# A transformer layer on one core: TensorE multiplies ones into an unread bank ahead of its first transposes and after its first token tile

## The chip, the cores and the metric

The kernel runs on one core of a Trainium2 chip. That core has four compute engines that run side by side, each with its own queue, worked off in order: TensorE (PE in the profile; its weight loads are PEld), VectorE (DVE), ScalarE (ACT) and GpSimd (POOL). A fifth queue, SyncE (SP), issues most DMA transfers. Engines wait for one another through semaphores. The metric is the device time of one execution in microseconds, as the median of several runs.

## The reference

One layer on 1024 tokens with 1024 features, in float32:

```python
h = rmsnorm(x, g_mix)
z = h @ w_in                     # pooling channels | q | k | v
y_pool = pool_mixer(z[pool])     # trailing means over 2, 4, 8, 16 tokens
y_attn = diff_attention(q, k, v) # 8 heads, two softmax maps each
gates  = sigmoid(h @ w_gate + b_gate)
x = x + (gates_1 * (y_pool @ w_branch_pool) + gates_2 * (y_attn @ w_branch_attn)) @ w_out
x = x + square(relu(rmsnorm(x, g_ffn) @ w_up)) @ w_down
```

Only the first two lines and the start of the attention's first head lie where the change is made; the rest matters since TensorE works through it behind them.

## The kernel before, in words

Every float32 matrix is split in two parts, a rounded "hi" and the remainder "lo". A product is then three multiplications: hi by hi, hi by lo, lo by hi (`mm3`, L126 to L128). The split (`split`) is a cast on ScalarE (L120), which writes hi, and a subtraction behind it (L121) on VectorE or GpSimd, which writes lo.

The tokens are cut into 8 tiles `t` of 128. For each tile, `norm_x` and `norm_transpose` square the row `x` and sum it (L244 for tile 0, L252 for the others, ScalarE), form the scale `rs` (VectorE L234, GpSimd L235), scale the row in two halves `hn` (VectorE L256), transpose each half by four TensorE transposes into a PSUM bank `hps` (L261), and split each bank by twos into `hT`: `hT0` and `hT1` come from the first half's bank, `hT2` and `hT3` from the second's. The splits are ScalarE casts L120 and VectorE subtractions L121 out of that bank.

`stage_qkv` then multiplies a tile with the q, k and v weights of one head into the bank `z`: eight steps `k` of three multiplications over 384 columns, 24 in all; steps 0 and 1 read `hT0`, 2 and 3 `hT1`, 4 and 5 `hT2`, 6 and 7 `hT3`. The weights of the first head come by DMA in four pieces `rqkv`, and are split into eight `wqkv`: eight casts on ScalarE, with the subtractions of numbers 0, 1, 4 and 5 on GpSimd, and of 2, 3, 6 and 7 on VectorE. `stage_prep` squares `z` (`sq`, ScalarE L423), reduces it (`ms`, VectorE L424) and scales it (`qn`, L428); later stages make scores, softmax and the product with v.

In the names of the instruction order, `hps1_0` is the first half's bank of tile 1, `z0_1` is head 0, tile 1, and the last number is only a serial number. `hT` has no tile in its name: its tiles hold four token tiles each, and the bank that is read tells which.

What the engines do in which order is not written out by hand. The program gives each instruction a priority, mostly its place in the source; a scheduler in the framework then plays the program with its own estimates of durations, and fixes for each engine the order in which instructions became ready there. Whatever takes time on one engine in that play can thus move instructions on all the others. On the chip each queue then runs in the fixed order.

## Time and profile before

| | us |
|---|---|
| time, median of 3 runs | 1529.52 (1528.83 to 1530.18) |
| the profiled execution's own time | 1529.71 |
| its span, first to last instruction | 1527.6 |
| TensorE busy | 1509.7 (99%) |
| VectorE, ScalarE, GpSimd busy | 1048.5, 804.7, 319.8 |
| TensorE's first multiplication starts | 8.75 |
| granted TensorE clock, mean over the span | 0.999 |

A row of the timeline holds the start, the time from the start of the first to the end of the last merged instruction, engine, line, operation, result and operands, the shape and the count, and in brackets how long the engine sat idle before and what ended that. Multiplications are pipelined: the distance from one start to the next is what one costs, not its duration. In rows of windows, each engine has its busy time and, in brackets, its instructions; PEclk is the clock that TensorE was granted, as a share of full speed.

### The profile page before, as it was taken

To read this page: it belongs to the slowest core of one execution; us is meant where nothing else is said; L and a number is where in the kernel's file an instruction comes from. 1 tells how busy PE (TensorE), PEld (TensorE's weight loads), DVE (VectorE), ACT (ScalarE), POOL (GpSimd) and SP (SyncE) were. 2 spreads that over 40 slices of the span, in tenths; PEclk is the share of its full clock that TensorE was granted. 3 is DMA by queue.
4 is the path that set the end of the run, shared out by engine and by line. 5 is a ranking of instruction groups with operands and counts; after the bars stand their busy time and mean duration, and the time that the engine had idled before them with its cause. 6 is when DMAs were issued, how large, how long until landed. Compare 5 with 4: busy or idle time off the path is not lost.

```text
span 1527.6 us, 21675 instructions
## 1 busy us (share of the span) xinstructions
PE 1509.7 (99%) x7441; PEld 1302.0 (85%) x7441; DVE 1048.5 (69%) x2262; ACT 804.7 (53%) x1693; POOL 319.8 (21%) x412
## 2 busy tenths in 40 slices
PE   7999999999999999999999999999999999999998
PEld 6999999999898989888888888888888888888887
DVE  6776668777777777746578559766665668556572
ACT  6665556656565565454464466555555634333331
POOL 6687333335234242312100011000000000000000
PEclk9999999999999999999999999999999999999999
DMA  7253202112112131627365734554433799537750
GB/s 247 100 159 120 76 29 62 51 44 66 43 44 84 49 98 40 223 89 254 120 209 191 248 104 149 169 178 152 148 128 110 274 344 383 170 125 262 228 190 28
DMA packets 171608, 221.07 MB, mean 145 GB/s; under 512 B 10902, under 2 KB 104811, under 8 KB 171499
## 3 DMA queue, kind: packets, MB, share of 16 engines
q1 hardware_dynamic: 154090, 192.39, 38.0%
q10 hardware_dynamic: 17408, 27.30, 4.8%
q8 instruction: 59, 0.97, 0.3%
q14 instruction: 51, 0.41, 0.1%
HBM read 157.76 MB, written 61.90 MB: 144 GB/s over the span
## 4 chain that ended last, share of the span: by engine, by line
PE 95%; DVE 2%; DMA 1%; ACT 1%; SPq 1%; issue 0%; POOL 0%; DVEq 0%
PE z L126 6%; PE z L128 6%; PE z L127 6%; PE Da L126 4%; PE Da L128 4%; PE Da L127 4%; PE g L126 4%; PE g L127 4%; PE g L128 4%; PE Db L126 3%; PE Db L128 3%; PE Db L127 3%; PE X L128 3%; PE X L127 3%; PE X L126 3%; PE sc L484 2%
## 5 line engine op out<-in xcount | busy, mean ns | idle before, releaser
L126 PE MATMUL z<-wqkv,hT 128*128 128x384 f32 x512 | 174.9, 343 | 0.6 <-DVE qn L428 0.4
L128 PE MATMUL z<-wqkv,hT 128*128 128x384 f32 x512 | 173.7, 340 | 0.0
L127 PE MATMUL z<-wqkv,hT 128*128 128x384 f32 x512 | 173.5, 339 | 0.0
L495 ACT ACTIVATE s<-s,nm 128x256 f32<-128x256 f32 (+7 forms) x128 | 99.5, 778 | 46.5 <-DVE nm L487 45.6
L126 PE MATMUL g<-hT,fwgate 128*128 128x512 f32 x256 | 101.1, 395 | 0.1
L127 PE MATMUL g<-hT,fwgate 128*128 128x512 f32 x256 | 100.8, 394 | 0.0
L128 PE MATMUL g<-hT,fwgate 128*128 128x512 f32 x256 | 100.5, 393 | 0.0
L126 PEld LDWEIGHTS z<-wqkv,hT 128*128 128x128 f32 x512 | 96.8, 189 | 3.4 <-DVE qn L428 0.6
L127 PEld LDWEIGHTS z<-wqkv,hT 128*128 128x128 f32 x512 | 96.9, 189 | 3.1 <-POOL wqkv L121 0.2
L235 POOL TENSOR_TENSOR ms<-ms,mhalf 128x4 f32<-128x4 f32 x64 | 65.7, 1027 | 158.3 <-DVE ms L234 135.3
L128 PEld LDWEIGHTS z<-wqkv,hT 128*128 128x128 f32 x512 | 96.5, 189 | 2.5 <-DVE hT L121 0.3
L121 DVE TENSOR_TENSOR AT<-ta,AT 128x256 fp32r<-128x256 f32 (+1 forms) x160 | 62.2, 392 | 32.7 <-ACT AT L120 31.6
L487 DVE CUSTOM_DVE_ANT_0 s<-sc,dist 128x512 f32<-128x512 f32 (+3 forms) x128 | 73.9, 583 | 13.2 <-PE sc L485 12.1
L120 ACT CAST AT<-ta 128x256 fp32r<-128x256 f32 (+1 forms) x160 | 54.5, 347 | 37.9 <-PE ta L527 23.1
L484 PE MATMUL sc<-K,Q 128*128 128x512 f32 (+2 forms) x192 | 69.8, 365 | 0.5 <-DVE nm L487 0.5
L121 DVE TENSOR_TENSOR AS<-s,AS 128x512 fp32r<-128x512 f32 x64 | 44.1, 693 | 36.5 <-ACT AS L120 36.3
L485 PE MATMUL sc<-K,Q 128*128 128x512 f32 (+2 forms) x192 | 66.4, 350 | 0.0
L121 POOL TENSOR_TENSOR wqkv<-rqkv,wqkv 128x384 fp32r<-128x384 f32 x60 | 61.8, 1044 | 19.8 <-ACT wqkv L120 16.7
L121 POOL TENSOR_TENSOR fwgate<-frgate,fwgate 128x512 fp32r<-128x512 f32 x32 | 43.3, 1356 | 66.0 <-ACT fwgate L120 66.0
L126 PEld LDWEIGHTS g<-hT,fwgate 128*128 128x128 f32 x256 | 48.1, 188 | 9.3 <-ACT go L730 0.5
L128 PEld LDWEIGHTS g<-hT,fwgate 128*128 128x128 f32 x256 | 48.1, 188 | 8.9
L127 PEld LDWEIGHTS g<-hT,fwgate 128*128 128x128 f32 x256 | 48.1, 188 | 8.4
(455 smaller groups left out, 4485.0 us busy)
## 6 DMA issues: line engine op xcount, KB each, us to landing
wd<-in_w_down_dram SPq DMA_DIRECT2D x56, 512.0 KB, 5.6
wu<-in_w_up_dram SPq DMA_DIRECT2D x32, 512.0 KB, 4.4
udS<-us SPq DMA_DIRECT2D x64, 256.0 KB, 2.4
ur<-udS SPq DMA_DIRECT2D x32, 512.0 KB, 3.4
rqkv<-in_w_in_dram SPq DMA_DIRECT2D x64, 192.0 KB, 2.7
ud<-u ACTq DMA_DIRECT2D x48, 256.0 KB, 4.1
ur<-ud SPq DMA_DIRECT2D x24, 512.0 KB, 4.3
frgate<-in_w_gate_dram SPq DMA_DIRECT2D x32, 256.0 KB, 2.8
```

What stands on the lines that cost most here:

```text
L120: nc.scalar.copy(hi, src)
L121: return (lo_eng or nc.vector).tensor_tensor(lo, src, f(hi), op=ALU.subtract)
L126: nc.tensor.matmul(ps, lhs_hi, rhs_hi, start=first, stop=False, **kw)
L127: nc.tensor.matmul(ps, lhs_hi, rhs_lo, start=False, stop=False, **kw)
L128: nc.tensor.matmul(ps, lhs_lo, rhs_hi, start=False, stop=last, **kw)
L235: nc.gpsimd.tensor_tensor(dst, dst, mhalf[:, :n], op=ALU.pow)
L484: nc.tensor.matmul(dst, Q[:, i, 0, :], rhs, start=True, stop=False)
L485: nc.tensor.matmul(dst, Q[:, i, 1, :], rhs, start=False, stop=True)
L487: nc.vector.tensor_tensor_reduce(out=s[i][:, c : c + w], in0=sc[:, 0:w], in1=dist[:, o0 + c : o0 + c + w], scale=2.0 ** -(h + 1), scalar=B ...
L495: nc.scalar.activation(s[i][:, 0:n], s[i][:, 0:n], AF.Exp, bias=last, scale=-1.0, accum_out=Z[:, i, t : t + 1])
```

## The change

A bank of the pool that later takes the attention's output is claimed early under the name `idle`. Nobody reads it. `keep_warm(n)` multiplies a 128x128 tile of ones into it n times, 512 columns each. It is called twice: with 22 ahead of everything that the start-up list `START` names, and with 7 behind the last multiplication of head 0, tile 0. `mm3` returns its last instruction for that purpose, and `issue_after` places the seven behind it.

```diff
-        nc.tensor.matmul(ps, lhs_lo, rhs_hi, start=False, stop=last, **kw)
+        return nc.tensor.matmul(ps, lhs_lo, rhs_hi, start=False, stop=last, **kw).ins
...
+        idle = ps_o.tile([P, 512], F32, tag="o", name="idle")
+
+        def keep_warm(n):
+            for _ in range(n):
+                nc.tensor.matmul(
+                    idle.rearrange("p (a b) -> p a b", a=4), ones, ones.unsqueeze(1).broadcast_to([P, 4, P]),
+                    start=True, stop=True,
+                )
+
+        keep_warm(22)
         for w in START.split():
...
-                mm3(z[:, 0:384], l_hi, l_lo, w[:, 0, :], w[:, 1, :], k == 0, k == NK - 1)
+                done = mm3(z[:, 0:384], l_hi, l_lo, w[:, 0, :], w[:, 1, :], k == 0, k == NK - 1)
+                if (h, t, k) == (0, 0, NK - 1):
+                    with tc.issue_after(done):
+                        keep_warm(7)
                 yield
```

The 29 multiplications are all that is added, and nothing is taken out. But the order moves on every engine, through the whole attention part (some 460 pieces of TensorE's order differ, nearly all within its first 4000 of 7441 multiplications). Three places matter to the prediction.

The first is ScalarE at the start, where it casts the first head's weights (`wqkv`) and tile 0's transposed rows (`hT` out of the banks `hps0_0` and `hps0_1`). Before:

```order
L120 CAST wqkv0_2_206<-rqkv0_1_189 128x384
L120 CAST hT0_0_0_150<-hps0_0_167 128x2x128
L120 CAST wqkv0_3_209<-rqkv0_1_189 128x384
L120 CAST wqkv0_4_214<-rqkv0_2_192 128x384
L120 CAST hT2_0_0_154<-hps0_1_177 128x2x128
L120 CAST hT1_0_0_152<-hps0_0_167 128x2x128
L120 CAST wqkv0_5_217<-rqkv0_2_192 128x384
L120 CAST wqkv0_6_220<-rqkv0_3_195 128x384
L120 CAST hT3_0_0_156<-hps0_1_177 128x2x128
L120 CAST wqkv0_7_223<-rqkv0_3_195 128x384
```

And now:

```order
L120 CAST wqkv0_2_229<-rqkv0_1_212 128x384
L120 CAST wqkv0_3_232<-rqkv0_1_212 128x384
L120 CAST wqkv0_4_237<-rqkv0_2_215 128x384
L120 CAST wqkv0_5_240<-rqkv0_2_215 128x384
L120 CAST hT0_0_0_173<-hps0_0_190 128x2x128
L120 CAST wqkv0_6_243<-rqkv0_3_218 128x384
L120 CAST hT2_0_0_177<-hps0_1_200 128x2x128
L120 CAST wqkv0_7_246<-rqkv0_3_218 128x384
L120 CAST hT1_0_0_175<-hps0_0_190 128x2x128
L120 CAST hT3_0_0_179<-hps0_1_200 128x2x128
```

The first cast of the rows moved behind three more weights, and `hT1`, which step 2 of the product reads, behind all eight.

The second is ScalarE from tile 1's square sum to tile 1's `hT1`. Before:

```order
L252 ACTIVATE hn1_248,ss1_249<-x1_198 128x1024
L252 ACTIVATE hn2_278,ss2_279<-x2_212 128x1024
L423 ACTIVATE sq0_0_431<-z0_0_372 128x256
L120 CAST hT0_0_0_150<-hps1_0_255 128x2x128
L120 CAST hT2_0_0_154<-hps1_1_265 128x2x128
L252 ACTIVATE hn3_304,ss3_305<-x3_226 128x1024
L120 CAST hT1_0_0_152<-hps1_0_255 128x2x128
```

And now:

```order
L252 ACTIVATE hn1_271,ss1_272<-x1_221 128x1024
L252 ACTIVATE hn2_301,ss2_302<-x2_235 128x1024
L436 ACTIVATE sq0_0_461<-z0_0_395 128x256
L391 ACTIVATE ls_264<-ls_264 128x2
L120 CAST hT0_0_0_173<-hps1_0_278 128x2x128
L120 CAST hT2_0_0_177<-hps1_1_288 128x2x128
L252 ACTIVATE hn3_327,ss3_328<-x3_249 128x1024
L252 ACTIVATE hn4_361,ss4_362<-x4_297 128x1024
L120 CAST hT0_0_0_173<-hps2_0_308 128x2x128
L120 CAST V0_0_391<-z0_0_395 128x128
L120 CAST hT1_0_0_175<-hps1_0_278 128x2x128
```

Tile 1's `hT1` moved behind tile 4's square sum, tile 2's `hT0` and the cast of v, and a small exponential (`ls`), whose operand VectorE reduces between the two halves of tile 2's `hn`, came ahead of tile 1's first cast.

The third is TensorE from the end of tile 0 to step 2 of tile 1. Before:

```order
L128 MATMUL z0_0_372<-wqkv0_7_223,hT3_0_1_157 128x384
L261 MATMUL hps1_0_255<-identf_96,hn1_248 128x128 x4
L261 MATMUL hps1_1_265<-identf_96,hn1_248 128x128 x4
L126 MATMUL z0_1_442<-wqkv0_0_200,hT0_0_0_150 128x384
L127 MATMUL z0_1_442<-wqkv0_0_200,hT0_0_0_150 128x384
L128 MATMUL z0_1_442<-wqkv0_0_200,hT0_0_1_151 128x384
L126 MATMUL z0_1_442<-wqkv0_1_203,hT0_0_0_150 128x384
L127 MATMUL z0_1_442<-wqkv0_1_203,hT0_0_0_150 128x384
L128 MATMUL z0_1_442<-wqkv0_1_203,hT0_0_1_151 128x384
L261 MATMUL hps2_0_285<-identf_96,hn2_278 128x128 x4
L126 MATMUL z0_1_442<-wqkv0_2_206,hT1_0_0_152 128x384
```

And now:

```order
L338 MATMUL idle_145<-ones_103 128x512 x7
L261 MATMUL hps1_0_278<-identf_96,hn1_271 128x128 x4
L261 MATMUL hps1_1_288<-identf_96,hn1_271 128x128 x4
L261 MATMUL hps2_0_308<-identf_96,hn2_301 128x128 x4
L126 MATMUL z0_1_472<-wqkv0_0_223,hT0_0_0_173 128x384
L127 MATMUL z0_1_472<-wqkv0_0_223,hT0_0_0_173 128x384
L261 MATMUL hps2_1_318<-identf_96,hn2_301 128x128 x4
L128 MATMUL z0_1_472<-wqkv0_0_223,hT0_0_1_174 128x384
L126 MATMUL z0_1_472<-wqkv0_1_226,hT0_0_0_173 128x384
L127 MATMUL z0_1_472<-wqkv0_1_226,hT0_0_0_173 128x384
L128 MATMUL z0_1_472<-wqkv0_1_226,hT0_0_1_174 128x384
L126 MATMUL z0_1_472<-wqkv0_2_229,hT1_0_0_175 128x384
```

The seven multiplications of ones stand between tile 0 and tile 1's transposes, and tile 2's first transposes moved ahead of all of tile 1's product.

## The prediction

> **What bounds the kernel now.** I read the page's busy times first, then TensorE's waits, the chain of waits at the start, and the timelines of the first 30 us.

> ```profile
> span 1527.6 us, 21675 instructions
> PE 1509.7 (99%) x7441; PEld 1302.0 (85%) x7441; DVE 1048.5 (69%) x2262; ACT 804.7 (53%) x1693; POOL 319.8 (21%) x412
> PE hps L261 <- DVE hn L256: 10.6, 2, 8.8
> PE X L128 <- DVE A L121: 0.9, 1, 0.9
> PE Y L126 <- DVE u L1246: 0.8, 1, 0.8
> PE Da L126 <- DVE u L1246: 0.5, 1, 0.5
> PE sc L484 <- DVE nm L487: 0.5, 1, 0.5
> PE z L126 <- DVE qn L428: 0.4, 1, 0.4
> ```

> The last six rows are TensorE's waits: total, times, longest. It waits 10.6 us for the first two tiles' rows and 0.9 + 0.8 + 0.5 + 0.5 + 0.4 = 3.1 us in all the rest. So from the second tile on the time is TensorE's own work, and each microsecond that TensorE starts this work later or wastes in it ends in the result.

> When that work starts is told by the chain of waits, and how fast by TensorE's timeline and three windows:

> ```profile
> 8.97 5.76 DMA x<-in_x_dram
> 14.75 1.16 ACT hn L252 x2
> ...
> 17.66 1.30 PE hps L261 x8
> ...
> 15.52 0.34 PE L128 MATMUL z<-wqkv,hT 128*128 128x384 f32 x1
> 18.75 0.69 PE L126 MATMUL z<-wqkv,hT 128*128 128x384 f32 x1
> 20.52 0.52 PE L128 MATMUL z<-wqkv,hT 128*128 128x384 f32 x1
> 20.84 1.05 PE L261 MATMUL hps<-identf,hn 128*128 128x128 f32 x4
> 21.55 0.67 PE L126 MATMUL z<-wqkv,hT 128*128 128x384 f32 x1
> 22.23 0.60 PE L261 MATMUL hps<-identf,hn 128*128 128x128 f32 x4
> 22.59 0.42 PE L128 MATMUL z<-wqkv,hT 128*128 128x384 f32 x1
> 23.02 0.34 PE L127 MATMUL z<-wqkv,hT 128*128 128x384 f32 x1
> 23.20 0.34 PE L128 MATMUL z<-wqkv,hT 128*128 128x384 f32 x1
> 26.84 1.47 PE L261 MATMUL hps<-identf,hn 128*128 128x128 f32 x12
> 28.07 0.42 PE L128 MATMUL z<-wqkv,hT 128*128 128x384 f32 x1
> ...
> 8.46:11.87 3.41, 3.12 (x12) 2.84 (x13) 2.65 (x5) 3.32 (x9) 2.81 (x3) 1.00 1.03 306
> 15.28:18.69 3.41, 1.61 (x12) 1.10 (x10) 2.08 (x7) 2.40 (x6) 0.87 (x2) 1.00 0.78 235
> 18.69:22.10 3.41, 3.41 (x14) 3.15 (x13) 3.19 (x12) 3.06 (x9) 3.26 (x5) 0.50 0.78 241
> ```

> Tile 1's row `x` lands at 14.75, and its norm lets the transposes start at 17.66. Tile 0's last multiplication started at 15.52 and ended at 15.86, so TensorE idles 1.8 us (15.86 to 17.66). Then it runs on, but from 18.69 to 22.10 at half clock (the last windows row, 0.50): six multiplications start from 18.75 to 20.84, 0.35 each at first and 0.32 at the end, where 23.02 to 23.20 shows 0.17 to 0.18.

> **The 22 ahead of the first transposes.** The ones are written early, and TensorE has nothing to do until the first half of `hn`:

> ```profile
> 0.90 0.20 POOL L218 MEMSET ones<- 128x128 f32 x1
> 8.75 1.97 PE L261 MATMUL hps<-identf,hn 128*128 128x128 f32 x8 [8.75 <-DVE hn L256]
> 32.30 0.39 PE L127 MATMUL g<-hT,fwgate 128*128 128x512 f32 x1
> 32.53 0.39 PE L128 MATMUL g<-hT,fwgate 128*128 128x512 f32 x1
> ```

> One of 512 columns costs 0.23 us at full clock (32.30 to 32.53); slow I take 0.32 x 512/384 = 0.43. From 1.1 on, 22 of them take 5.1 us if all are fast and 9.5 if all are slow. The slow stretch seen lasted 3.41 us, and where the switches fall need not be tied to the kernel's start; 8 slow and 14 fast give 1.1 + 3.4 + 3.2 = 7.7, before 8.75. At worst they run to 10.6 and push the transposes.

> Would that matter, or would earlier, faster transposes help? ScalarE answers both:

> ```profile
> 8.47 1.62 ACT L120 CAST wqkv<-rqkv 128x384 fp32r<-128x384 f32 x3 [4.17 <-DMA rqkv<-in_w_in_dram]
> 9.99 0.37 ACT L120 CAST hT<-hps 128x256 fp32r<-128x256 f32 x1
> 10.26 1.00 ACT L120 CAST wqkv<-rqkv 128x384 fp32r<-128x384 f32 x2
> 11.16 0.64 ACT L120 CAST hT<-hps 128x256 fp32r<-128x256 f32 x2
> 9.06 5.07 POOL L121 TENSOR_TENSOR wqkv<-rqkv,wqkv 128x384 fp32r<-128x384 f32 x4 [3.08 <-DMA rqkv<-in_w_in_dram]
> ```

> Before, three weights, then `hT0` at 9.99, ready at 10.36, and TensorE's first product at 10.41; `hT2` and `hT1` end at 11.80. A weight costs about 0.5, a row piece about 0.3. In the new order six weights precede `hT0`: 8.47 + 6 x 0.5 = 11.5, ready at 11.85, even if the transposes end as late as 11.4. So the speed of the first transposes buys nothing, and the product starts 1.45 later. `hT1` then comes behind `hT0`, a weight, `hT2` and a weight: 11.5 + 2 x 0.35 + 2 x 0.5 = 13.2, ready at 13.5 against 11.8. Its lo half, on VectorE behind three weights and two row pieces, I put at 14.6. From step 2's third multiplication there are 16 left, 16 x 0.17 = 2.8: tile 0 ends at 17.4, if slow for part of it 17.8, against 15.86. The fixed bound of before, GpSimd's subtractions until 14.13 (9.06 + 5.07), is no longer the last.

> **The seven after tile 0.** 7 x 0.23 = 1.6 us: 17.4 + 1.6 = 19.0, or 19.4. Tile 1's transposes, whose operand is ready at 17.6, so start 1.3 to 1.7 late. With tile 0 ending as before, at 15.9, they would end at 17.5 and cost nothing, under the cover of tile 1's norm.

> **Tile 1 behind them.** Here the moved order of ScalarE decides:

> ```profile
> 19.27 1.06 ACT L252 ACTIVATE hn<-x 128x1024 f32<-128x1024 f32 x1
> 20.32 0.36 ACT L120 CAST hT<-hps 128x256 fp32r<-128x256 f32 x1
> 20.57 1.07 ACT L252 ACTIVATE hn<-x 128x1024 f32<-128x1024 f32 x1
> 18.16 0.41 DVE L424 TENSOR_REDUCE ms<-sq 128x4 f32<-128x256 f32 x1
> 19.22 1.41 DVE L256 SCALAR_TENSOR_TENSOR hn<-x,rs,gmb 128x512 f32<-128x512 f32 x2
> 20.55 0.28 DVE L380 TENSOR_REDUCE ls<-lp 128x2 f32<-128x128 f32 x1
> ```

> VectorE starts the reduction `ms` of tile 0 at 18.16 before; now two small products stand ahead of it, which I put at 0.4. Behind them come `ms` (0.4), one half of `hn2` (0.7) and `ls` (0.2 to the next start): 19.85. ScalarE's exponential waits for that, 0.2: 20.05. Then `hT0` and `hT2` of tile 1 (20.75), the square sums of tiles 3 and 4 at 1.05 each (19.27 to 20.32): 22.8, `hT0` of tile 2 and v, 0.5, and `hT1` of tile 1 at 23.3, ready at 23.65. TensorE meanwhile does the transposes of tile 1 and tile 2 and steps 0 and 1 of tile 1, and is through at 22.2 to 22.5. It waits 1.2 to 1.4 us for `hT1`, behind which all the rest queues, whenever tile 0 ended. Step 2's first two run to 24.0. The same set of work was done before at 22.59: **1.4 us late.**

> After that the rows carry it: tile 2's product waits until `qn` of tile 0 has left its bank (I put it at 24.15), and by 29.6 TensorE has done what it had done at 28.07: 1.5 late. The stretch at half clock, in which the kernel before lost 6 x 0.15 = 0.9 on products, 0.35 on four transposes (20.84 to 21.55 against 22.23 to 22.59) and 0.3 on step 2 (two in 0.68, 21.55 to 22.23), is already inside this difference: the saving of 1.5 is real, and the late start (1.3 to 1.7) and the wait (1.2 to 1.4) eat it twice.

> Later, nothing is added. By the order the multiplications that stand between a tile's product and its transposes of q and k are 15 us of work at the least (12 before), and the groups of transposes 171 for 175, so I cost the moved remainder at nothing, between 3.1 less (all other waits gone) and 3.1 more (twice the waits).

> Sum: 1529.71 + 1.5 = 1531.2 for the profiled execution; the median lay 0.2 under it: **1531.0**.

> [...]

> **The rivals.**

> *It does what it says.* If the casts on ScalarE are early enough after all, transposes start at 17.66, no half clock follows, and 1.5 are saved: 1528.0. For it: the stretch of 0.50 is there to be saved. Against: two places of ScalarE's order. 18%.

> *The clock falls again.* The new wait before step 2 leaves TensorE idle for up to 1.4 us. In the window that fell, 1.61 of 3.41 were busy, transposes included, and it was followed by 3.4 us at half. If 22.2 to 23.6 lies in one window, about 1.9 of 3.41 are busy, not much more. Then another 1.6 are lost: 1532.6. [...] 15%; a little over half of it beyond 0.2%.

> *The moved remainder costs.* One mechanism: a square sum of a coming tile, or another early item, ahead of a cast that TensorE waits for, as at tile 1, on later tiles and heads. At 3.1 more: 1534.1, slower. Against it stands the cover above. 10%.

> *The moved remainder gains,* with the saving whole: down to 1529.5 - 1.5 - 3.1 = 1524.9. 5%.

> **How the numbers follow.** My forecast has 52%. A measurement of this kernel can tell about 0.2%, 3.1 us, from no change: 1526.5 to 1532.6 counts as the same. That holds the forecast (but for 2%), the first rival and less than half of the second: 0.74. Slower: 0.02 + 0.09 + 0.10 = 0.21. Faster: 0.05. The range from 1527.4 to 1533.3 leaves out most of the third and all of the fourth rival, some 13%, and a few per cent at the edges.

> **What would show it.** In the changed profile: the multiplications of ones end before 8.7; ScalarE's first `hT` cast starts near 11.5; tile 0's last product near 17.4; the seven end near 19; TensorE waits over 1 us before step 2 of tile 1, until about 23.6; no window at 0.50 between 18 and 22. The 12 transposes that began at 26.84 end 1.5 us later. It is wrong if the transposes of tile 1 start by 17.7, if a second stretch at half clock shows, or if TensorE's waits behind 30 us add up to much other than 3 us.

## The result, and the profile after

The changed kernel takes 1537.91 us (median of 6 runs, 1536.59 to 1538.21) against 1529.41 us for the kernel before (6 runs, 1528.35 to 1530.18): a ratio of 1.0054, with a 95% interval from 1.0041 to 1.0067. It is slower by 8.5 us. The forecast was 1531.0, within 1527.4 to 1533.3.

The page of the changed kernel, span and busy times, and then all of TensorE's waits of 0.8 us and more (total, times, longest):

```profile
span 1535.5 us, 21743 instructions
PE 1520.0 (99%) x7470; PEld 1308.5 (85%) x7470; DVE 1044.9 (68%) x2262; ACT 809.3 (53%) x1693; POOL 320.1 (21%) x412
PE z L126 <- ACT hT L120: 3.4, 2, 2.1
PE z L126 <- DVE qn L441: 1.6, 2, 1.3
PE idle L338 <- POOL ones L218: 1.2, 1, 1.2
PE hps L261 <- DVE hn L256: 1.0, 1, 1.0
PE X L128 <- DVE A L121: 0.9, 1, 0.9
PE Y L126 <- DVE u L1259: 0.8, 1, 0.8
```

The 10.6 us of waiting for the first two tiles' rows are down to 1.0, because the ones fill the first of these waits and a later end of tile 0 the second. In their place stand 3.4 us for casts of `hT` on ScalarE, a wait that the kernel before did not have, and 1.6 us for `qn` on VectorE, where it was 0.4. TensorE is busy 10.3 us longer (1520.0 for 1509.7), and the ones alone take 6.7 + 1.8 = 8.5 of that, as the next rows show.

TensorE's timeline at the start of the changed kernel:

```profile
1.16 6.71 PE L338 MATMUL idle<-ones 128*128 128x512 f32 x22 [1.16 <-POOL ones L218]
8.85 1.32 PE L261 MATMUL hps<-identf,hn 128*128 128x128 f32 x8 [0.99 <-DVE hn L256]
12.26 0.69 PE L126 MATMUL z<-wqkv,hT 128*128 128x384 f32 x1 [2.09 <-ACT hT L120]
17.40 0.52 PE L126 MATMUL z<-wqkv,hT 128*128 128x384 f32 x1
17.72 0.41 PE L127 MATMUL z<-wqkv,hT 128*128 128x384 f32 x1
...
19.03 0.33 PE L128 MATMUL z<-wqkv,hT 128*128 128x384 f32 x1
19.20 1.78 PE L338 MATMUL idle<-ones 128*128 128x512 f32 x7
20.82 1.47 PE L261 MATMUL hps<-identf,hn 128*128 128x128 f32 x12
25.11 0.44 PE L126 MATMUL z<-wqkv,hT 128*128 128x384 f32 x1 [1.32 <-ACT hT L120]
31.84 0.42 PE L128 MATMUL z<-wqkv,hT 128*128 128x384 f32 x1
```

Tile 0's product starts at 12.26, behind a wait of 2.09 us for the first cast, and up to 17.72 one multiplication costs 0.32 us (17.40 to 17.72), the half-clock price. It ends at 19.4 (19.03 + 0.33). The seven follow, tile 1's transposes start at 20.82, and before step 2 of tile 1 TensorE waits 1.32 us more. The last row is the multiplication that started at 28.07 before: here it starts at 31.84, **3.8 us late**. The span is 7.9 us longer in all, so another **4.1 us** are lost later.

The windows of the changed kernel, with the granted clock as the third number from the end:

```profile
10.00:15.00 5.00, 2.91 (x11) 2.42 (x9) 4.59 (x8) 4.67 (x12) 4.19 (x4) 0.60 1.02 364
15.00:20.00 5.00, 5.00 (x21) 4.87 (x21) 2.42 (x8) 1.65 (x5) 1.85 (x4) 0.71 0.80 273
```

The half-clock stretch has not gone. It moved from 18.69:22.10 to the time from about 11 to 17.8, and became twice as long: at 0.5 the first row's 0.60 means 4.0 us at half clock, the second row's 0.71 means 2.9 us.

ScalarE's timeline of the changed kernel shows what the first product and step 2 of tile 1 waited for:

```profile
8.57 3.36 ACT L120 CAST wqkv<-rqkv 128x384 fp32r<-128x384 f32 x6 [4.58 <-DMA rqkv<-in_w_in_dram]
11.84 0.37 ACT L120 CAST hT<-hps 128x256 fp32r<-128x256 f32 x1
...
19.40 0.39 ACT L436 ACTIVATE sq<-z 128x256 f32<-128x256 f32 x1 [3.13 <-PE z L128]
21.13 0.20 ACT L391 ACTIVATE ls<-ls 128x2 f32<-128x2 f32 x1 [1.34 <-DVE ls L390]
24.66 0.94 ACT L120 CAST hT<-hps 128x256 fp32r<-128x256 f32 x3
```

Six weight casts stand ahead of the first `hT`, which starts at 11.84 instead of 9.99. And at 19.40 ScalarE has been idle for 3.13 us, waiting for the end of tile 0's product; all that follows, down to tile 1's `hT1`, hangs on that end.

Behind 30 us the largest single wait that the kernel before did not have is at 123 us. TensorE's, VectorE's and GpSimd's timelines of the changed kernel:

```profile
119.20 1.02 POOL L235 TENSOR_TENSOR ms<-ms,mhalf 128x4 f32<-128x4 f32 x1 [0.99 <-DVE ms L234]
121.42 1.27 DVE L517 SCALAR_TENSOR_TENSOR s<-s,cf,s 128x1024 f32<-128x1024 f32 x1
122.61 0.41 DVE L441 TENSOR_TENSOR qn<-z,ms 128x256 f32<-128x256 f32 x1
123.17 0.41 PE L126 MATMUL z<-wqkv,hT 128*128 128x384 f32 x1 [1.26 <-DVE qn L441]
```

`qn` of head 1, tile 3 reads the bank `z` and so frees it for a later product. What it needs from GpSimd is there at 120.2, but in VectorE's order it stands behind the 1.27 us combination of two softmax maps (L517, head 0, tile 7). TensorE waits 1.26 us for the bank.

### The profile page after: what moved, and what is told of

Same layout as the page of the kernel before. It is cut to its first block, busy times and chain, and to the rows that moved or that the text cites. A ratio compares the mean times of both kernels' runs of the same rounds, so it can differ in the third digit from the quotient of the medians.

```text
span 1535.5 us, 21743 instructions
## 1 busy us (share of the span) xinstructions
PE 1520.0 (99%) x7470; PEld 1308.5 (85%) x7470; DVE 1044.9 (68%) x2262; ACT 809.3 (53%) x1693; POOL 320.1 (21%) x412
## 4 chain that ended last, share of the span: by engine, by line
PE 91%; DVE 4%; DMA 1%; ACT 1%; issue 1%; SPq 1%; POOL 0%; ACTq 0%; DVEq 0%
PE z L126 5%; PE z L128 5%; PE z L127 5%; PE Da L126 4%; PE Da L127 4%; PE Da L128 4%; PE g L126 4%; PE g L127 4%; PE g L128 3%; PE Db L127 3%; PE Db L128 3%; PE Db L126 3%; PE X L128 3%; PE X L126 3%; PE X L127 3%; PE sc L497 2%
## 5 line engine op out<-in xcount | busy, mean ns | idle before, releaser
L126 PE MATMUL z<-wqkv,hT 128*128 128x384 f32 x512 | 174.6, 342 | 5.2 <-ACT hT L120 3.4
L127 PE MATMUL z<-wqkv,hT 128*128 128x384 f32 x512 | 174.7, 341 | 0.0
L128 PE MATMUL z<-wqkv,hT 128*128 128x384 f32 x512 | 174.0, 341 | 0.0
L126 PEld LDWEIGHTS z<-wqkv,hT 128*128 128x128 f32 x512 | 97.0, 189 | 10.0 <-ACT hT L120 4.0
L126 PE MATMUL g<-hT,fwgate 128*128 128x512 f32 x256 | 100.7, 393 | 0.5 <-ACT yps L735 0.5
L127 PE MATMUL g<-hT,fwgate 128*128 128x512 f32 x256 | 100.8, 394 | 0.0
L128 PE MATMUL g<-hT,fwgate 128*128 128x512 f32 x256 | 100.8, 394 | 0.0
L127 PEld LDWEIGHTS z<-wqkv,hT 128*128 128x128 f32 x512 | 97.0, 190 | 3.3
L128 PEld LDWEIGHTS z<-wqkv,hT 128*128 128x128 f32 x512 | 96.9, 189 | 2.4 <-DVE hT L121 0.3
L500 DVE CUSTOM_DVE_ANT_0 s<-sc,dist 128x512 f32<-128x512 f32 (+3 forms) x128 | 74.5, 584 | 12.7 <-PE sc L498 11.6
L121 DVE TENSOR_TENSOR AT<-ta,AT 128x256 fp32r<-128x256 f32 (+1 forms) x160 | 61.8, 391 | 25.9 <-ACT AT L120 25.0
L120 ACT CAST AT<-ta 128x256 fp32r<-128x256 f32 (+1 forms) x160 | 55.0, 349 | 41.5 <-PE ta L540 24.2
L121 DVE TENSOR_TENSOR AS<-s,AS 128x512 fp32r<-128x512 f32 x64 | 44.2, 694 | 36.7 <-ACT AS L120 36.6
L121 POOL TENSOR_TENSOR wqkv<-rqkv,wqkv 128x384 fp32r<-128x384 f32 x60 | 63.4, 1077 | 21.3 <-ACT wqkv L120 17.7
L121 POOL TENSOR_TENSOR fwgate<-frgate,fwgate 128x512 fp32r<-128x512 f32 x32 | 45.0, 1409 | 58.0 <-ACT fwgate L120 52.2
L128 PEld LDWEIGHTS g<-hT,fwgate 128*128 128x128 f32 x256 | 48.0, 188 | 8.9
L126 PEld LDWEIGHTS g<-hT,fwgate 128*128 128x128 f32 x256 | 48.1, 188 | 8.8 <-ACT yps L735 0.7
L127 PEld LDWEIGHTS g<-hT,fwgate 128*128 128x128 f32 x256 | 48.1, 188 | 8.2
```

Of the source, the lines that this page charges most:

```text
L120: nc.scalar.copy(hi, src)
L121: return (lo_eng or nc.vector).tensor_tensor(lo, src, f(hi), op=ALU.subtract)
L126: nc.tensor.matmul(ps, lhs_hi, rhs_hi, start=first, stop=False, **kw)
L127: nc.tensor.matmul(ps, lhs_hi, rhs_lo, start=False, stop=False, **kw)
L128: return nc.tensor.matmul(ps, lhs_lo, rhs_hi, start=False, stop=last, **kw).ins
L500: nc.vector.tensor_tensor_reduce(out=s[i][:, c : c + w], in0=sc[:, 0:w], in1=dist[:, o0 + c : o0 + c + w], scale=2.0 ** -(h + 1), scalar=B ...
```

## The experiments

In most of them the order is written out: the kernel holds one table per engine and ties each instruction to its neighbour by an edge without a semaphore, so that nothing but the place in the queue is set. In the tables a number counts an engine's instructions as the source names them; `f22` are 22 multiplications of ones. These kernels have other line numbers: L553 are the transposes, L418 to L420 the multiplications of `mm3`, L412 and L413 the split, L630 the ones, L733 `qn`. "Before" is 1529.7 us in all the comparisons (17 to 20 runs each).

### The ones alone, in the order of before

```diff
+        for one, two in zip(row, row[1:]):
+            tc.add_manual_dep(two, one.name, edge, reason="in_order")
...
+    "PE": (
+        "f22 0-7 40-63 f7 8-15 72-77 16-19 78-79 20-23 80-91 107-112 92-95 113-114 24-35 115-126 2793 36-39 127-130 "
```

> All 29 multiplications of ones stay, at the same two places of TensorE's queue; edges between neighbours pin every engine's order to the one of the kernel before. Theory A (the moved order makes the loss, the multiplications themselves save the half clock): about 1528.0, 1.5 us under before, no stretch at half clock from 18 to 22 us, tile 1's transposes at 17.7. Theory B (the multiplications cost: they hold TensorE, or the clock falls whatever they do): 1531 to 1537, with tile 1's transposes late or a stretch at half clock.

Measured: 1529.30 us (11 runs, 1528.61 to 1532.05), ratio 0.9999 with 0.9990 to 1.0008. TensorE's timeline:

```profile
1.16 8.09 PE L630 MATMUL idle<-ones 128*128 128x512 f32 x22 [1.16 <-POOL ones L510]
10.34 0.44 PE L418 MATMUL z<-wqkv,hT 128*128 128x384 f32 x1 [0.22 <-ACT hT L412]
15.61 1.78 PE L630 MATMUL idle<-ones 128*128 128x512 f32 x7
17.25 1.23 PE L553 MATMUL hps<-identf,hn 128*128 128x128 f32 x8
26.95 0.42 PE L420 MATMUL z<-wqkv,hT 128*128 128x384 f32 x1
```

With the same 29 multiplications and the old order nothing is lost. In this execution the seven fit into the gap, no stretch at half clock follows (granted clock 1.00 in the windows from 15 to 25 us, 0.17 us from one multiplication to the next, 22.00 to 22.17), and the multiplication of 28.07 starts at 26.95: 1.1 us are saved. In the medians 0.4 us remain, too little to be told from nothing, and the median lies 1.3 us above what the theory expected. So the 8.5 us do not come from the ones. That the ones spare the half clock in general is not shown: an execution with the same start, under "Where in the remainder", had such a stretch all the same.

### The change's order without any ones

```diff
-        keep_warm(22)
...
-                if (h, t, k) == (0, 0, NK - 1):
-                    with tc.issue_after(done):
-                        keep_warm(7)
...
+    "PE": (
+        "0-7 40-63 8-19 72-73 20-23 74-79 107-112 80-95 113-114 24-35 115-123 36-39 124-130 2793-2798 143-145 148-152 "
```

> No multiplications of ones; every engine's order pinned to the one of the changed kernel. Theory A: nearly all of the loss stays, 1536 to 1537.5 (the seven fall away, worth up to 1.6 us, but tile 1 waits for ScalarE all the same). Theory B: back to 1529 to 1531.

Measured: 1537.37 us (5 runs, 1536.80 to 1539.45), ratio 1.0046 with 1.0033 to 1.0060. The loss is the order's: it is there, to 0.5 us, with no multiplication of ones in the program. (The profiled execution is the slowest of the five; the last section shows a half clock that is part of the reason.)

### The start or the remainder

Two hybrids, both with all 29 multiplications: the first 30 us (103 of TensorE's own multiplications, and what the other engines issue by then) in the change's order and all the rest in that of before, and the reverse. Against the first experiment 34 instructions of TensorE, 28 of VectorE and 19 of ScalarE stand elsewhere in the former; 3285, 997 and 811 in the latter. The start of TensorE's table in the former:

```diff
-        "f22 0-7 40-63 f7 8-15 72-77 16-19 78-79 20-23 80-91 107-112 92-95 113-114 24-35 115-126 2793 36-39 127-130 "
+        "f22 0-7 40-63 f7 8-19 72-73 20-23 74-79 107-112 80-95 113-114 24-35 115-126 2793 36-39 127-130 2794-2808 "
```

> All 29 multiplications; the instructions that the kernel before had started by 30 us stand in the changed kernel's order, everything behind them in the order of the kernel before. If the two parts add up: the changed trace is 3.8 us late at the 12 transposes near 30 us, so about 1533.2, 3.8 above before. If the late start is what spoils the rest: about 1537. If TensorE's rest has slack for it: under 1531.

> All 29 multiplications; the first 30 us in the order of the kernel before, everything behind in the changed kernel's order. If the two parts add up: the saving of 1.5 us at the start and the other 4.1 us of the loss: about 1532. If the moved remainder costs nothing by itself: about 1528. My prediction's step that cost it at nothing stands or falls here.

Measured: the change's start alone 1533.91 us (7 runs), ratio 1.0025 with 1.0014 to 1.0036; the change's remainder alone 1535.09 us (5 runs), ratio 1.0034 with 1.0022 to 1.0047. Against 1529.30 for the ones in the old order the start costs 4.6 us and the remainder 5.8. The start lies 0.7 us above the time expected for it, the remainder 3.1 above the 1532 that was expected if the parts add up. Their sum is 10.4, both together cost 8.6: which would fit a late start that covers some of the remainder's waits, but each interval is nearly 2 us wide to either side, so the medians could also differ by chance. Neither part is nothing. Which is the larger the intervals do not tell.

### Only tile 0's order

Of the change's order only what is issued in the first 15.9 us. On TensorE and GpSimd nothing moves; 9 instructions of ScalarE and 7 of VectorE do. ScalarE's table (5 to 12 are the eight weight casts, 1 to 4 `hT0` to `hT3`):

```diff
-        "0 5-7 1 8-9 3 2 10-11 4 12 14 19 40 15 17 24 16 29 41 20 13 18 22 39 21 23 858-859 47-48 25 27 34 30 26 42 28 "
+        "0 5-10 1 11 3 12 2 4 14 19 40 15 17 24 16 29 41 20 13 18 22 39 21 23 858-859 47-48 25 27 34 30 26 42 28 31-32 "
```

> All 29 multiplications; only what the kernel before had started by 15.9 us (tile 0's casts, subtractions and product) stands in the changed kernel's order, all else in the old one. If the first of my two places, tile 0's casts behind the weights, carries the start's loss of 4.2 us: about 1533, tile 1's transposes near 20.5. If the second place, tile 1's casts behind two square sums, carries it: about 1530.5.

Measured: 1533.16 us (10 runs, 1531.68 to 1537.18), ratio 1.0025 with 1.0016 to 1.0034: 3.9 us above the ones in the old order. By its size this would be most of the start's 4.6, as expected for tile 0's casts. The trace shows another loss. One of TensorE's waits and three rows of its timeline:

```profile
PE z L418 <- ACT hT L412: 1.7, 1, 1.7
...
29.77 0.63 PE L553 MATMUL hps<-identf,hn 128*128 128x128 f32 x4 [1.95 <-DVE hT L413]
30.71 0.52 PE L419 MATMUL z<-wqkv,hT 128*128 128x384 f32 x1
31.03 0.52 PE L420 MATMUL z<-wqkv,hT 128*128 128x384 f32 x1
```

Tile 0's product waits 1.7 us for the cast behind six weights, but it runs at full pace (0.17 us from one multiplication to the next, 15.22 to 15.39), and tile 1's transposes start at 18.75, not near 20.5 as expected. A second wait of 1.95 us follows at 29.77, in a piece that has the order of before: in that order it did not exist as long as tile 0 was on time. Behind it the multiplications are 0.32 us apart, from 30.71 up to 32.95 at the least. The changed kernel has neither: its wait at that place is 0.44 us (at 31.46), and the multiplications behind it are 0.17 us apart (32.10 to 32.27). So these 16 places, moved alone, cost 3.9 us, but the median met the expected 1533 by luck, and what share of the start's loss in the change is theirs is not shown.

### The gap before tile 0's product filled

The change's order with nine more multiplications of ones between tile 0's transposes and its product:

```diff
-        keep_warm(22)
+        keep_warm(31)
...
-        "f22 0-7 40-63 f7 8-19 72-73 20-23 74-79 107-112 80-95 113-114 24-35 115-123 36-39 124-130 2793-2798 143-145 "
+        "f22 0-7 f9 40-63 f7 8-19 72-73 20-23 74-79 107-112 80-95 113-114 24-35 115-123 36-39 124-130 2793-2798 143-145 "
```

> The changed kernel's order, pinned, with nine more multiplications of ones between tile 0's transposes and its product, where TensorE sat idle from 10.2 to 12.3 us. Theory (that gap lets the clock fall, and half clock until 17.8 carries the part of the late start that I had not counted): no half clock in tile 0, its last product near 17.5 rather than 19.0, tile 1's transposes near 19.3, and 1.0 to 1.6 us under the changed kernel: about 1536.5. If the clock falls all the same or the chain through ScalarE holds tile 1 as long: 1537.9.

Measured: 1535.72 us (4 runs), ratio 1.0041 with 1.0027 to 1.0054; 2.2 us less than the change, where 1.0 to 1.6 were expected. A window and three rows of TensorE's timeline:

```profile
10.00:15.00 5.00, 4.20 (x19) 2.74 (x18) 4.72 (x8) 3.85 (x11) 4.14 (x4) 1.00 0.98 337
...
17.86 1.79 PE L630 MATMUL idle<-ones 128*128 128x512 f32 x7
23.76 0.45 PE L418 MATMUL z<-wqkv,hT 128*128 128x384 f32 x1 [1.31 <-ACT hT L412]
29.87 0.42 PE L420 MATMUL z<-wqkv,hT 128*128 128x384 f32 x1
```

The clock stays at 1.00 (0.17 us from one multiplication to the next, 17.34 to 17.51), tile 0 ends 1.3 us earlier (the seven start at 17.86 for 19.20), and the multiplication of 28.07 starts at 29.87: 1.8 late. The four executions show a mean granted clock of 0.999 or 1.000, the six of the change 0.997 to 0.999. By these two traces, 2.0 of the 3.8 us at the start are the half clock and 1.8 the order.

### `qn` ahead of the long combination

The change's order and ones, with one instruction of VectorE moved: `qn` of head 1, tile 3 (229) from behind L516 and L517 of head 0, tile 7 (217 and 203) to a place ahead of them.

```diff
-        "211 195 192 198 193-194 206 264 196 207 199 226 228 197 200 227 215-216 201 204 202 217 203 229 205 212 220 "
+        "211 195 192 198 193-194 206 264 196 207 199 226 228 197 200 227 215-216 201 204 229 202 217 203 205 212 220 "
```

> The changed kernel's order, pinned, but VectorE scales head 1, tile 3 (the write of qn) ahead of the last tile of head 0's difference of the two softmax maps, not behind it. Theory (one such swap is what a microsecond of the moved remainder consists of): TensorE's wait of 1.3 us at 123 us is gone, and the time is 1.0 to 1.3 under the changed kernel: about 1536.7. If the wait has another cause: it stays, 1537.9.

Measured: 1535.58 us (4 runs, 1534.70 to 1537.02), ratio 1.0043 with 1.0028 to 1.0058. The long wait is gone; a row of its timelines, and the window at its start:

```profile
120.15 0.42 DVE L733 TENSOR_TENSOR qn<-z,ms 128x256 f32<-128x256 f32 x1 [0.45 <-PE tk L751]
...
15.00:20.00 5.00, 5.00 (x26) 4.64 (x27) 3.39 (x11) 1.64 (x5) 1.98 (x4) 0.92 0.84 246
```

`qn` now runs at 120.15 instead of 122.61. The kernel gained 2.3 us, more than the 1.3 of the wait. In the profiled execution the half-clock stretch at the start, where nothing was edited, was also shorter (0.92 in this window against 0.71), so the excess need not be the edit's. The two traces bear this out: TensorE's 601st multiplication besides the ones, ahead of the wait, starts 1.0 us earlier than in the changed kernel (120.23 for 121.28), the 785th, behind it, 2.4 earlier (152.79 for 155.24). So the wait came from that one place of `qn`, and its removal was worth about 1.4 us in these executions.

### Where in the remainder

Two more hybrids with all 29 multiplications, both with the start of before: the change's order from 30 to about 150 us only, and from about 150 us on only. TensorE's table at the seam near 30 us in the former:

```diff
-        "f22 0-7 40-63 f7 8-15 72-77 16-19 78-79 20-23 80-91 107-112 92-95 113-114 24-35 115-126 2793 36-39 127-130 "
+        "f22 0-7 40-63 f7 8-15 72-77 16-19 78-79 20-23 80-91 107-112 92-95 113-114 24-35 115-123 36-39 124-130 "
```

> Before's order up to 30 us, the change's order from there to about 150 us (784 multiplications), before's order behind, with all 29 multiplications of ones. The change's order behind 30 us cost 5.7 us of span in the run that had it alone (1532.2 against 1526.5). Theory 'a few named places': VectorE's qn behind a 1.27 us instruction near 122 us is the largest single one, TensorE's idle time from 40 to 160 us grew by 1.5 us there, so 2 to 3 us of the 5.7 lie in this piece: span 1528.5 to 1529.5, median 1531.3 to 1532.3. Rival 'it lies evenly over the attention part': 120 of 670 us, 1.0 us: span 1527.5, median 1530.3. Rival 'it is all at the seam near 30 us and just behind it': 5.7: span 1532, median 1535.

> The mirror: before's order for the first 784 multiplications (about 150 us), the change's order behind, with all 29 multiplications of ones. Theory 'a few named places': 2.7 to 3.7 us of the 5.7 are left: span 1529.2 to 1530.2, median 1532 to 1533. 'Evenly over the attention part': 4.7 are left: span 1531.2, median 1534. 'All near 30 us': nothing is left: span 1526.5, median 1529.3.

Measured: 30 to 150 us alone 1533.48 us (7 runs, 1531.53 to 1535.66), ratio 1.0030 with 1.0019 to 1.0041; behind 150 us alone 1531.98 us (11 runs, 1530.49 to 1534.28), ratio 1.0016 with 1.0007 to 1.0024. Both were measured on another chip than the first experiment, where the kernel before took the same 1529.74. Against 1529.30 that is 4.2 and 2.7 us. TensorE's waits and idle time in the former (here L416 and L731 are the first multiplication and `qn`), and the window from 280 to 340 us in the latter:

```profile
PE z L416 <- DVE qn L731: 2.1, 3, 1.2
100.00:160.00 60.00, 58.05 (x335) 53.48 (x334) 42.00 (x136) 35.04 (x96) 44.41 (x62) 1.00 0.43 140
```

```profile
280.00:340.00 60.00, 59.38 (x329) 53.63 (x329) 44.10 (x140) 35.99 (x95) 24.99 (x31) 1.00 0.22 69
```

The same window with the ones in the order of before:

```profile
280.00:340.00 60.00, 60.00 (x337) 54.78 (x336) 46.61 (x147) 36.80 (x100) 23.23 (x29) 1.00 0.18 55
```

"Evenly over the attention part" would have been 1530.3 and 1534.0, and fails on both. "Near 30 us" would have been 1535 and 1529.3, and fails on the second. "A few named places" expected 1531.3 to 1532.3 and 1532 to 1533: it misses the first by 1.2 us and the second lies at its lower end, so no expectation fits both. The loss is denser in the first 120 us, where the `qn` wait and 2.0 us of idle time in one window (60.00 - 58.05) lie, and goes on in places behind: in the window from 280 to 340 us TensorE is idle for 0.6 us, where it is busy for the whole 60.00 in the old order.

The changed kernel's own trace can be set against that of the kernel before wherever both orders have the same work behind them. Besides the ones, its 93rd multiplication is 3.8 us late (31.84 for 28.07), its 785th 5.2 (155.24 for 150.04), its 3226th 8.1 (595.72 for 587.67) and its last 7.9. So 1.4 us are lost between 30 and 150 us, about as much as the wait for `qn` is long, 2.9 between 150 and 590 us, and nothing behind. What the 2.9 consist of is open: the longest new wait that the trace names there is 0.5 us.

The profiled execution of the latter run is the slowest of its eleven, and it lost time where nothing was moved. Up to 150 us its order is that of the first experiment, ones included:

```profile
10.00:15.00 5.00, 3.69 (x15) 2.92 (x14) 4.16 (x8) 4.31 (x11) 4.07 (x4) 0.77 0.99 324
...
30.21 0.42 PE L420 MATMUL z<-wqkv,hT 128*128 128x384 f32 x1
```

ScalarE got its first weights 0.9 us later (first cast at 9.30 for 8.40), the clock was halved from 12.7 to 16.1, and the multiplication of 28.07 started at 30.21, 3.3 us later than in the first experiment. So the same start can save 1.1 us or lose 2.1.

### Another count of ones

The change itself with 16 instead of 22, and no order written out. On TensorE, VectorE, GpSimd and SyncE the scheduler then gives the order of before; on ScalarE two casts change places (`hT2` ahead of a weight).

```diff
-        keep_warm(22)
+        keep_warm(16)
```

> The changed kernel with 16 ones in place of 22 and nothing pinned. The order then is that of the kernel before on TensorE, VectorE, GpSimd and SyncE, and differs in one pair of ScalarE's casts. Theory (the order makes the loss, by what the scheduler is given, not by what TensorE executes): 1528.5 to 1529.5, about 8 us under the changed kernel. If the count itself mattered, 7 of 29 multiplications fewer would give at most 22 to 16 x 0.23, 1.4 us, back: 1536.5.

Measured: 1529.14 us (11 runs, 1527.55 to 1531.11), ratio 0.9998 with 0.9989 to 1.0007. Six multiplications fewer, and the 8.5 us are gone.

### 22 alone, seven alone

The order of before with one of the two calls left out, each in a single execution.

```diff
-        "f22 0-7 40-63 f7 8-15 72-77 16-19 78-79 20-23 80-91 107-112 92-95 113-114 24-35 115-126 2793 36-39 127-130 "
+        "f22 0-7 40-63 8-15 72-77 16-19 78-79 20-23 80-91 107-112 92-95 113-114 24-35 115-126 2793 36-39 127-130 "
```

> Before's order, only the 22 multiplications ahead of the first transposes, none behind tile 0. Theory 'the gap between tile 0 and tile 1 is what the clock falls in': TensorE idles about 1.8 us before tile 1's transposes near 17.4, half clock for 3.4 us behind them, span near 1527.6 as before. Rival 'being busy before 8.7 us is enough to carry the clock over that gap': no stretch at half clock, span near 1526.5.

> Before's order, only the 7 multiplications behind tile 0. Theory 'the gap is what the clock falls in': no stretch at half clock from 15 to 30 us, span near 1526.5, the whole saving. Rival 'the 22 carry it': a stretch at half clock in spite of the seven, span near 1527.6.

Measured: spans of 1527.0 us with the 22 and 1528.2 us with the seven. Executions of the kernel before range from 1525.3 to 1529.0, so single spans tell nothing here. The rows do tell something. With the 22 alone, window and TensorE's timeline:

```profile
10.00:15.00 5.00, 3.67 (x14) 2.97 (x13) 4.54 (x8) 4.09 (x11) 3.36 (x4) 0.75 1.01 348
...
1.16 7.42 PE L630 MATMUL idle<-ones 128*128 128x512 f32 x22 [1.16 <-POOL ones L510]
10.75 0.44 PE L418 MATMUL z<-wqkv,hT 128*128 128x384 f32 x1 [0.55 <-ACT hT L412]
17.67 1.23 PE L553 MATMUL hps<-identf,hn 128*128 128x128 f32 x8
```

The gap before tile 1's transposes did not open in this execution: tile 0's last multiplication starts at 17.49, the transposes at 17.67. So it tells nothing of what the theory expected there. A stretch at half clock stands at 12 to 16 us instead (0.32 us from one multiplication to the next, 12.66 to 12.98), which neither theory expected. The first experiment had the same program up to there and no such stretch, the run with the change's order behind 150 us had the same start and did. What differs is that its 22 ran until 9.25 (1.16 + 8.09) and its product began at 10.34, where these ran until 8.58 and the product began at 10.75. With the seven alone no stretch at half clock shows between 15 and 30 us (1.00 in its windows). Whether either call protects the clock, and in how many executions, stays open.

## Why the prediction was wrong, and where it was right

**The 22.** Right: they run from 1.16 to 7.87, where 7.7 was forecast, and delay nothing.

**The new place of `hT0`.** Right in kind and nearly in size: behind six weights it starts at 11.84 (forecast 11.5), and the product at 12.26 (forecast 11.85).

**Tile 0's product.** Mis-sized. The forecast let it end at 17.4, or 17.8 if slow for a part; it ended at 19.4. TensorE waited 2.09 us for the late cast, the granted clock fell to 0.50 within that wait, at about 11 us, and 16 multiplications then ran at half clock. The forecast had the wait, and had a rival in which the clock falls in a new wait; but it looked for that at step 2 of tile 1, from 22 to 24 us, and not at the first and longest new wait. With the gap filled, the clock stayed at 1.00 and the seven start at 17.86, just behind the forecast's 17.8.

**The wait before step 2 of tile 1.** Right in length: 1.32, forecast 1.2 to 1.4. Wrong in "whenever tile 0 ended": ScalarE's square of `z` at 19.40 was released by that end, and the whole row behind it moved along, to 25.11 instead of 23.65. With the gap filled it ended at 23.76.

**The start in all.** The term of 1.5 measured 3.8 in the profiles: 1.8 from the order, as forecast within 0.3, and 2.0 from the half clock. The saving that the forecast counted inside its 1.5 was not there either, since half clock was not spared but moved.

**The clock.** What the prediction had was one trace: 1.8 us of idling, and half clock behind it. In the changed kernel TensorE had only eight transposes to do from 7.87 to 12.26, 4.4 us, and half clock stood from about 11 to 17.8. With the 22 alone in the old order it had only the transposes from 8.58 to 10.75, 2.2 us, then a wait of 0.78 us in the product, and half clock stood from about 12.5 to 15.9. In the order without ones, 1.97 us without any multiplication were followed by half clock (last section). Waits of 1.32 us in the changed kernel (to 25.11) and of 1.66 us with only tile 0's order (to 11.46) were followed by none. A length of idling from which the clock falls is not shown. In these executions the 22 multiplications gained nothing ahead of a product that late: it runs at half pace until 17.72 in the changed kernel, and until 17.66 in the same order without ones.

**"Later, nothing is added."** This is the step that failed by most. The moved remainder was costed at nothing, with 3.1 us as the most it could lose; alone it costs 5.8 us (4.1 in the trace of the change behind the late start). A sign that the prediction had set for this showed: TensorE's waits behind 30 us add up to 5.5 us in the changed kernel, where it named 3. The cover that the prediction counted, work between a tile's product and its transposes of q and k, was not where the loss lay: at 123 us a later product waited for its *bank*, because `qn`, which frees it, stood behind a 1.27 us instruction of another head. The third rival came near in kind (an early item ahead of a cast that TensorE waits for, 1534.1 at most; here it was a long item of the head before, ahead of a read that frees a bank) and had too little weight, and its bound of "twice the waits" was taken from a kernel whose waits the order had already made small. That bound says nothing about another order of 3319 moved multiplications.

**The range** held neither of the two losses together. Each alone would have lain beyond its upper end of 1533.3: 1533.9 for the start, 1535.1 for the remainder.

## What to carry to other kernels

Where a scheduler lays down the order by its own durations, filler is not neutral: 22 ones in place of 16 cost 8.8 us through instructions that have nothing to do with them. Look at what an addition moves on every engine before judging what it does, and either choose an amount that leaves the order alone or write the order down. An order that has moved has no bound in the waits of the old one; sixteen places on two engines, moved alone, cost 3.9 us here.

## What the runs showed of the hardware

```profile
10.00:15.00 5.00, 3.57 (x13) 2.86 (x11) 4.64 (x8) 3.74 (x11) 4.12 (x4) 1.00 1.03 355
...
13.97 0.52 PE L420 MATMUL z<-wqkv,hT 128*128 128x384 f32 x1
14.29 0.52 PE L418 MATMUL z<-wqkv,hT 128*128 128x384 f32 x1
```

They are 0.32 us apart, as at half clock, in a window marked 1.00. The multiplications of this trace are 0.32 us apart up to 17.66 and 0.18 from 18.19 on, and the window from 15 to 20 us is marked 1.00 as well. The 1.00 of the kernel before from 8.46 to 11.87 is of the same kind: its products at 10.90, 11.22 and 11.55 are 0.32 us apart, those at 11.87 and 12.04 0.17. The first entry of the granted clock in its trace stands at 11.86 and says full speed; ahead of it there is none, and the view then shows 1.00. At the start of these executions the distance between starts is therefore the safer sign.

Half clock followed a wait of 1.97 us far from the start, too. In the trace of the order without ones, a row and two windows:

```profile
123.59 0.43 PE L418 MATMUL z<-wqkv,hT 128*128 128x384 f32 x1 [1.97 <-DVE qn L720]
...
120.45:123.86 3.41, 1.44 (x10) 1.23 (x9) 2.96 (x9) 2.85 (x10) 1.58 (x4) 1.00 0.22 77
123.86:127.27 3.41, 3.41 (x12) 3.41 (x11) 2.65 (x10) 1.46 (x5) 3.41 (x6) 0.50 0.46 164
```

TensorE was busy for 1.44 of 3.41 us, and 3.41 us at half clock followed, as after 1.61 of 3.41 in the kernel before. By an estimate from these rows the half clock took another 1.7 us (half of 3.41) behind the wait; this execution was 2.1 us above the median of its kernel. In the changed kernel the same wait was 1.26 us, and no half clock followed.

Being busy did not bring the clock back at once: in the changed kernel the product ran without a break from 12.26, yet at half pace until 17.72, 5.5 us. And the stretch that the change was set against, half clock from 18.69 to 22.10, is not in every execution, as far as the granted clock shows it. Of 54 executions of the kernel before, 16 show a mean granted clock of 0.999 (median span 1527.95 us) and 38 show 1.000 (1527.4 us); the profiled execution was one of the 16. So the saving of 1.5 us, read from that one, may have been mostly absent from the median to begin with.
